# A small-tile pool moved to the bottom of SBUF, and ScalarE's work regrouped where two MLP phases meet

## The chip, the cores and the metric

The kernel runs on one core of a Trainium2 chip. The metric is the device time of one execution in microseconds (us). The engines are TensorE (PE; its weight loads, PEld, run beside the matmuls), VectorE (DVE), ScalarE (ACT), GpSimd (POOL) and SyncE (SP). On the last two mostly DMAs are issued; every engine works its own instructions off in order. On-chip memory (SBUF) has 128 partitions; an address below is a byte offset within a partition. Matmul results go to PSUM.

## The reference, cut to what matters

Two layers over 1024 tokens of width 1024, in float32. The change lies in the MLP of each layer; its pool edit moves operands of all matmuls.

```python
for i in range(DEPTH):                      # DEPTH = 2
    h = rms_norm(x, norm_mix_g[i])
    ...                                     # projections, convolution, retention
    x = x + mix                             # mix = [conv_out, ret_out] @ w_out[i]
    h = rms_norm(x, norm_ffn_g[i])
    x = x + jnp.square(jax.nn.relu(h @ w_ff1[i])) @ w_ff2[i]     # 1024 -> 4096 -> 1024
    h = rms_norm(x, norm_ple_g[i])
    x = x + jax.nn.sigmoid(h @ w_ple_gate[i]) * (p[i] @ w_ple_proj[i])
return rms_norm(x, final_norm_g)
```

## The kernel before

**Products.** Each float32 operand is split into a high part (rounded, made by ACT: `split`, L220) and a low part (the rest, made by DVE, L221), and a product is three matmuls (`mm3`, L252 to L254). A row of the profile such as `ps_mm<-h,s_hi` names the result, then the moving operand (512 columns that stream through the array), then the stationary one (128x128, loaded ahead).

**The MLP.** Both matrix products are done in 2x2 blocks by the seven-product (Strassen-Winograd) scheme. In the first phase `ff1_pair` makes a pair of hidden blocks at a time, p = 0 to 15: five products on sums of blocks of h and of the weights (two more were done early), then relu and square on ACT (L655, L656, the function `act`), then differences of the squared blocks on DVE, the *forms*, which go to DRAM by POOL (`store`, L658). The last pair, p = 15, belongs to a chunk that is done plainly later, and stores its squares only.

In the second phase `ff2_pairs` reads the forms back chunk by chunk (j = 0 to 6): `fetch` (L712, on POOL) brings the seven forms of a chunk into a ring of eleven tiles, and `ready` splits them on ACT and DVE. For each of four column groups g, `begin` does the first product into a PSUM tile p (`ps_ret`, two buffers), copies it to q on ACT (`copy(q, p)`, L744), and the other products go on from p, q and three further PSUM tiles e, y, r. The second product into p has to wait for that copy.

**The boundary.** While the last pair runs, `hook` already fetches chunk 0 and makes the first four of its forms ready. ACT therefore works on the last pair's squares, on chunk 0's splits, on the first weights of phase two and on the first `begin` in one queue.

**Who sets the order.** Instructions are written in the order of the code; a list scheduler then orders each engine's queue by priority. `issue_after(x)` adds the rule that the instructions of the block on x's engine stand behind x.

**Pools.** SBUF pools lie one above the other in the order in which they are opened: const, stage, w_hi, w_lo, h, tmp, small, and above these the pools of a stage, which are opened and closed (at, hx, s_hi, s_lo, ft; then form, acc; later pp, pr). small holds ten kinds of tiny tiles, three buffers each, padded to 32 bytes: 1,152 bytes, which is 4 x 256 + 128. In the built program stage begins at address 57,728 (225 x 256 + 128) and the pools of a stage at 153,088 (598 x 256). All tiles of stage, w_hi, w_lo, h and tmp are 2, 4 or 8 KB, so each of them begins 128 bytes past a multiple of 256; each tile of at, hx, s_hi, s_lo, ft, form, acc, pp and pr begins at a multiple of 256.

Of the kernel before, what the change touches and what calls it, by code (L numbers as in the profile page):

```python
# [43 lines left out]
PAIRS = D // (2 * P)  # L44
# [8 lines left out]
T_OUT, T_FF1, T_FF2, T_GATE, T_PROJ = 24, 32, 64, 96, 104  # L53
# [19 lines left out]
class _Trunk:  # L73
    def __init__(self, ctx, tc, x, xT, pT, pos, wts, vecs, convw, tabs, outT):
        self.tc, self.nc = tc, tc.nc
        self.x_tok, self.xT, self.pT, self.pos, self.wts = x, xT, pT, pos, wts
        self.vecs, self.convw, self.tabs, self.outT = vecs, convw, tabs, outT
        pool = lambda name, bufs, **kw: ctx.enter_context(tc.tile_pool(name=name, bufs=bufs, **kw))
        psum = bass.MemoryType.PSUM
        self.const = pool("const", 1)  # L80
        self.pools = {
            "stage": pool("stage", 2),
            "w_hi": pool("w_hi", 2),
            "w_lo": pool("w_lo", 2),
            "h": pool("h", 8),
            "tmp": pool("tmp", 2),
            "small": pool("small", 3),
            "ps_mm": pool("ps_mm", 5, space=psum),
            "ps_ret": pool("ps_ret", 2, space=psum),
            "ps_aux": pool("ps_aux", 1, space=psum),  # L90
        }

        self.small([P, 1], "pad")
        self.right = ctx.enter_context(ExitStack())
        self.norm_pools()
        self.dram = pool("dram", 1, space=bass.MemoryType.DRAM)
        self.low = {}
# [551 lines left out]
    def ff1_pair(self, L, p, xf, ws, e, early, forms, hook):  # L649
        nc, copy, add, sub = self.nc, self.nc.scalar.copy, self.nc.vector.tensor_add, self.nc.vector.tensor_sub  # L650
        t1, t2, t3, t4, q22 = xf
        w, sa, sb = ws

        def act(r, ps):
            nc.scalar.activation(r, ps, AF.Relu)  # L655
            nc.scalar.activation(r, r, AF.Square)  # L656

        store = lambda f, n, t: nc.gpsimd.dma_start(out=forms[p // 2][:, f:f + n, p % 2, :], in_=t)  # L658
        more = p + 1 < NPAIR
        b = self.tile("ps_mm")  # L660
        copy(b, e[0])  # L661
        self.product(b, sa, 0, t2, False, part=True)
        c = self.tile("ps_mm")
        copy(c, b)
        hook(p, 0)
        ps = self.tile("ps_ret")
        self.product(ps, sa, HT, t1, True)
        es = self.tile("tmp")
        copy(es, ps)
        hook(p, 1)  # L670
        if more:
            nxt = self.ff1_weights(L, p + 1)
            next(nxt)
            ne = self.early_load(p + 1, early)
        self.product(b, sb, 0, t3, False, part=True)
        qs = self.ft()
        q21, q22o = qs[:, 0, :], qs[:, 1, :]
        add(q22o, b, es)
        act(q22o, q22o)
        hook(p, 2)  # L680
        self.product(c, sb, HT, q22, False, part=True)
        q12 = es
        add(q12, c, es)
        act(q12, q12)
        hook(p, 3)
        if more:
            ws = next(nxt)
        self.product(b, w, HT, t4, False, part=True)
        act(q21, b)
        store(0, 2, qs)  # L690
        if p // 2 < WIDE:
            ta, tb = self.ft(), self.ft()
            sub(ta[:, 0, :], q12, e[1])
            sub(tb[:, 1, :], q22o, q12)
            sub(ta[:, 1, :], q22o, ta[:, 0, :])
            store(2, 2, ta)
            sub(tb[:, 0, :], q21, ta[:, 1, :])
            store(4, 2, tb)
        else:
            store(2, 1, q12)  # L700
        hook(p, 4)
        return (ws, ne) if more else None

    def slot(self):
        q = self.ring[self.turn % len(self.ring)]
# [24 lines left out]
            self.split(s, sh, sl)  # L730
        return (hi, lo), (sh, sl)

    def ff2_pairs(self, L, sources):
        nc, add, copy = self.nc, self.nc.vector.tensor_add, self.nc.scalar.copy
        acc_e, acc_h = (self.pools["acc"].tile([P, PAIRS, HT], F32, name="acc") for _ in range(2))
        self.acc = acc_e, acc_h

        def begin(j, g, ws):
            e = self.tile("ps_mm")
            if j:  # L740
                copy(e, acc_e[:, g, :])
            p, q = self.tile("ps_ret"), self.tile("ps_mm")
            self.product(p, ws[0], 2 * P, forms[0], True, part=True)
            copy(q, p)  # L744
            return e, p, q, ws[0], ws[1]

        weights = self.pair_weights(L, T_FF2)
        forms = self.coming
        now = begin(0, 0, weights)
        for j in range(WIDE):  # L750
            plain = j + 1 == WIDE
            for g in range(PAIRS):
                e, p, q, w, s = now
                q11, t1, t2, q21, t4, t3, q22 = forms
                end = g + 1 == PAIRS
                x11, x12 = self.x[2 * g]
                x21 = self.x[2 * g + 1][0]
                y = self.tile("ps_mm")
                copy(y, x21)
                self.product(e, s, 0, t1, j == 0, part=j > 0)  # L760
                copy(acc_e[:, g, :], e)
                if g == 0:
                    self.ready(*((4, 5, 6) if j == 0 else (6,)))
                    self.coming = []
                    self.fetch(sources[j + 1][:4])
                if end and not plain:
                    self.fetch(sources[j + 1][5:6])
                self.product(p, s, 2 * P, t2, False, part=True)
                r = self.tile("ps_mm")
                copy(r, p)  # L770
                if end and not plain:
                    self.fetch(sources[j + 1][6:7])
                self.product(q, w, 4 * P, q21, False, part=True)
                add(x11, x11, q)
                if 0 < g < 3:
                    self.ready(2 * g - 2)
                self.product(y, w, 6 * P, t4, False, part=True)
                copy(x21, y)
                if 0 < g < 3:
                    self.ready(2 * g - 1)  # L780
                if end and not plain:
                    self.ready(4)
                self.product(p, s, 4 * P, t3, False, part=True)
                if j:
                    add(acc_h[:, g, :], acc_h[:, g, :], p)
                else:
                    copy(acc_h[:, g, :], p)
                if end:
                    forms = self.coming
                if not (end and plain):  # L790
                    ng = (g + 1) % PAIRS
                    now = begin(j + end, ng, self.pair_weights(L, T_FF2 + PAIRS * (j + end) + ng))
                if g == 2 and not plain:
                    self.fetch(sources[j + 1][4:5])
                self.product(r, s, 6 * P, q22, False, part=True)
                add(x12, x12, r)
                if end and not plain:
                    self.ready(5)
        return self.coming
# [65 lines left out]
    def run(self):  # L865
# [8 lines left out]
        for L in range(DEPTH):  # L874
# [12 lines left out]
            with self.stage_pools(gen=16, conv_acc=4, ret=4, ctmp=3, rtmp=2, u=3):  # L887
# [15 lines left out]
                q = self.proj_qk(L, 0, hs, T_Q)  # L903
# [13 lines left out]
                q = self.proj_qk(L, 1, hs, T_Q)  # L917
# [11 lines left out]
            sources = []  # L929
            for j in range(NFB):  # L930
                q11 = early[j][:, :, 1, :]
                q21, q22s, t1s, t2s, t4s, t3s = (forms[j][:, f] for f in range(6))
                sources.append([q11, t1s, t2s, q21, t4s, t3s, q22s] if j < WIDE else [q11, q21, t1s, q22s])

            def hook(p, at):
                if p + 1 == NPAIR:
                    if at == 0:
                        self.fetch(sources[0][0:2])
                    elif at == 1:
                        self.fetch(sources[0][2:4])  # L940
                    elif at == 2:
                        self.fetch(sources[0][4:5])
                        self.ready(0)
                    elif at == 3:
                        self.fetch(sources[0][5:7])
                        self.ready(1)
                    else:
                        self.ready(2, 3)

            self.right_pools(ntmp=4, rstd=2)  # L950
            with self.stage_pools(at=2, hx=2, s_hi=2, s_lo=2):
                with self.stage_pools(ft=7):
# [24 lines left out]
                    now = ws, e  # L977
# [3 lines left out]
                        now = self.ff1_pair(L, p, (t1, t2, t3, t4, q22), *now, early, forms, hook)  # L981
                with self.stage_pools(form=1, acc=2):
                    self.ring[8] = self.pools["form"].tile([P, 4, HT], F32R, name="form")
                    f = self.ff2_pairs(L, sources)
                    self.norm_pools()
                    self.merge_pairs(0)
                    self.ff2(L, NFB - 1, 0, f[:2])
                    self.merge_pairs(1)
                    h3A = self.norm(0, v0 + V_PLE, SLACK)
                    self.ff2(L, NFB - 1, 1, f[2:])  # L990
# [94 lines left out]
```

## Time and profile before

| | before |
|---|---|
| median of three runs | 2378.33 us (2377.74 to 2378.80) |
| the profiled execution: its time / its span | 2378.69 us / 2376.7 us |
| PE busy | 2314.1 us, 97% of the span |
| DVE / ACT / POOL busy | 78% / 53% / 10% |
| mean granted TensorE clock | 0.994 of full speed |
| last pair of layer 0 ends, phase two begins | at about 748 us of the span |
| the same in layer 1 | at about 1919 us |

Time outside the span is 2.0 us. A busy PE is not a PE at its peak: a matmul's duration in a row (0.39 us) overlaps the next one's, so the pace is read from the distance of starts. A row of the timeline is: start, duration, engine, line, operation, `out<-in`, shapes, count, and in brackets the idle time of the engine just before and what ended it.

### The profile page before, as it was taken

The numbers are of one execution on the slowest core, as the hardware profiler recorded it, in microseconds if no ns is written. First come the engines' busy times: TensorE is split into PE (matmuls) and PEld (weight loads), VectorE is DVE, ScalarE is ACT, GpSimd is POOL, SyncE is SP. The second block draws the span as 40 slices with busy tenths as digits, with TensorE's granted clock in tenths as the row PEclk, the third lists the DMA queues.
The fourth block names the chain that finished last, engine by engine and source line by source line (L and its number), as shares of the span: only waits on it lengthen the run. The fifth ranks groups of instructions, "written<-read, shape, count | busy, mean of one in ns | idle before, by whom it ended". The sixth has DMA issues, their size and how long they took to land.

```text
span 2376.7 us, 29537 instructions
## 1 busy us (share of the span) xinstructions
PE 2314.1 (97%) x10548; PEld 1886.0 (79%) x10548; DVE 1857.8 (78%) x3262; ACT 1267.6 (53%) x2090; POOL 231.9 (10%) x364
## 2 busy tenths in 40 slices
PE   8999999999999999999999999999999999999998
PEld 7887887778887878788888888777788877777887
DVE  8999997376666677878999889845766667777788
ACT  5335237365556676736542352464655567676454
POOL 1000011001221101000000100100022111010000
PEclk9999999999999999999999999999999999999999
DMA  7644544666666444422265454555566654343324
GB/s 271 194 160 150 172 149 163 227 199 204 219 233 239 141 151 138 155 72 88 89 195 180 149 171 156 175 196 187 191 218 233 237 194 164 126 162 120 89 80 151
DMA packets 119171, 403.29 MB, mean 170 GB/s; under 512 B 13216, under 2 KB 21408, under 8 KB 119024
## 3 DMA queue, kind: packets, MB, share of 16 engines
q1 hardware_dynamic: 64032, 220.75, 30.5%
q0 software_dynamic: 43472, 157.59, 18.6%
q10 hardware_dynamic: 11520, 23.07, 2.6%
q8 instruction: 82, 1.34, 0.2%
q14 instruction: 65, 0.53, 0.1%
HBM read 295.46 MB, written 105.91 MB: 169 GB/s over the span
## 4 chain that ended last, share of the span: by engine, by line
PE 63%; issue 20%; DVE 8%; DMA 3%; POOL 3%; ACT 3%; POOLq 0%; DVEq 0%; ACTq 0%
PE ps_mm L252 19%; PE ps_mm L253 19%; PE ps_mm L254 19%; DVE conv_acc L411 2%; PE ps_ret L252 2%; PE ps_ret L254 2%; PE ps_ret L253 2%; POOL h L712 1%; DMA stage<-in_wts_dram 1%; DVE w_lo L221 1%; DVE h L221 1%; POOL gn_rs L546 1%; DMA w_lo<-low 1%; DMA h<-forms 1%; DVE ntmp L277 0%
## 5 line engine op out<-in xcount | busy, mean ns | idle before, releaser
L252 PE MATMUL ps_mm<-h,w_hi 128*128 128x512 f32 (+1 forms) x1584 | 615.2, 388 | 8.6 <-ACT w_hi L241 4.2
L254 PE MATMUL ps_mm<-h,w_lo 128*128 128x512 f32 (+1 forms) x1584 | 611.5, 386 | 2.9 <-DMA w_lo<-low 2.7
L253 PE MATMUL ps_mm<-h,w_hi 128*128 128x512 f32 (+1 forms) x1584 | 613.0, 387 | 0.0
L220 ACT CAST w_hi<-stage 128x1024 fp32r<-128x1024 f32 (+2 forms) x240 | 226.6, 944 | 300.1 <-PE ps_mm L253 169.7
L252 PEld LDWEIGHTS ps_mm<-h,w_hi 128*128 128x128 f32 x1584 | 299.2, 189 | 69.3 <-ACT w_hi L241 6.1
L254 PEld LDWEIGHTS ps_mm<-h,w_lo 128*128 128x128 f32 x1584 | 299.3, 189 | 62.8 <-DMA w_lo<-low 3.5
L253 PEld LDWEIGHTS ps_mm<-h,w_hi 128*128 128x128 f32 x1584 | 299.6, 189 | 56.1
L411 DVE SCALAR_TENSOR_TENSOR conv_acc<-u,cw,conv_acc 128x512 f32<-128x512 f32 x480 | 334.6, 746 | 0.9
L221 DVE TENSOR_TENSOR w_lo<-stage,w_hi 128x1024 fp32r<-128x1024 f32 (+2 forms) x240 | 261.1, 1088 | 51.0 <-ACT w_hi L220 50.3
L252 PE MATMUL ps_mm<-h,s_hi 128*128 128x512 f32 x400 | 158.9, 397 | 4.5 <-ACT ps_mm L661 4.5
L253 PE MATMUL ps_mm<-h,s_hi 128*128 128x512 f32 x400 | 158.5, 396 | 0.0
L254 PE MATMUL ps_mm<-h,s_lo 128*128 128x512 f32 x400 | 158.0, 395 | 0.0
L252 PE MATMUL ps_mm<-w_hi,h 128*128 128x512 f32 x384 | 150.6, 392 | 0.0
L253 PE MATMUL ps_mm<-w_lo,h 128*128 128x512 f32 x384 | 150.3, 391 | 0.0
L254 PE MATMUL ps_mm<-w_hi,h 128*128 128x512 f32 x384 | 150.2, 391 | 0.0
L241 ACT CAST w_hi<-stage 128x1024 fp32r<-128x1024 f32 x64 | 67.5, 1054 | 154.4 <-PE ps_mm L253 80.7
L270 ACT ACTIVATE ntmp<-x 128x256 f32<-128x256 f32 x208 | 81.1, 413 | 84.7 <-DVE ntmp L277 32.2
L252 PE MATMUL ps_ret<-h,s_hi 128*128 128x512 f32 x272 | 110.0, 405 | 16.5 <-ACT ps_mm L744 14.4
L221 DVE TENSOR_TENSOR s_lo<-ft,s_hi 128x1024 fp32r<-128x1024 f32 x64 | 78.4, 1225 | 52.7 <-ACT s_hi L220 52.7
L221 DVE TENSOR_TENSOR h<-h 128x1024 fp32r<-128x1024 f32 x76 | 92.6, 1222 | 30.8 <-ACT h L220 30.4
L254 PE MATMUL ps_ret<-h,s_lo 128*128 128x512 f32 x272 | 108.4, 398 | 0.0
L253 PE MATMUL ps_ret<-h,s_hi 128*128 128x512 f32 x272 | 108.0, 397 | 0.0
(267 smaller groups left out, 4310.1 us busy)
## 6 DMA issues: line engine op xcount, KB each, us to landing
stage<-in_wts_dram SPq DMA_DIRECT2D x336, 512.0 KB, 4.2
forms<-ft POOLq DMA_DIRECT2D x88, 512.0 KB, 6.2
low<-w_lo POOLq DMA_DIRECT2D x64, 512.0 KB, 5.2
w_lo<-low SPq DMA_DIRECT2D x64, 512.0 KB, 3.3
h<-forms POOLq DMA_DIRECT2D x62, 512.0 KB, 6.0
early<-at ACTq DMA_DIRECT2D x32, 512.0 KB, 4.4
at<-early POOLq DMA_DIRECT2D x30, 512.0 KB, 4.2
hx<-forms POOLq DMA_DIRECT2D x18, 512.0 KB, 5.7
```

The lines of the kernel that those rows point to most:

```text
L220: self.nc.scalar.copy(hi, src)
L221: self.nc.vector.tensor_sub(lo, src, hi.bitcast(F32))
L241: self.nc.scalar.copy(hi, st)
L252: mm(ps, lhsT=wh, rhs=xh, start=start, stop=False)
L253: mm(ps, lhsT=wh, rhs=xl, start=False, stop=False)
L254: mm(ps, lhsT=wl, rhs=xh, start=False, stop=stop)
L270: square = lambda k, out: nc.scalar.activation(out, self.x[k][h][:, cs], AF.Square)
L411: nc.vector.scalar_tensor_tensor(acc, u[:, j:j + HT], w(j), acc, ALU.mult, ALU.add)
L546: nc.gpsimd.tensor_tensor(rs, rs, self.npow[:, 0:HEADS], ALU.pow)
L712: self.nc.gpsimd.dma_start(out=f[1].bitcast(F32), in_=src)
```

## The change

1. The pool small is opened before stage instead of behind tmp. In the built program stage then begins at 58,880 (230 x 256), h at 83,456 (326 x 256); the pools of a stage stay at 153,088. Nothing else moves.
2. In the last pair, the square of q12, the relu and square of q21 and both their stores are taken out of `ff1_pair` and returned as a function `rest`. The other square, q22o, is stored alone at once (so two stores become three), and q21's square goes to a tile of the pool tmp instead of ft.
3. `ff2_pairs` calls `rest` behind its first `begin`, under `issue_after` the copy L744 (L758 in the change). Chunk 0's late forms, `ready(4, 5, 6)`, get the same rule.

```diff
         self.pools = {
+            "small": pool("small", 3),
             "stage": pool("stage", 2),
             "w_hi": pool("w_hi", 2),
             "w_lo": pool("w_lo", 2),
             "h": pool("h", 8),
             "tmp": pool("tmp", 2),
-            "small": pool("small", 3),
             "ps_mm": pool("ps_mm", 5, space=psum),
...
         q12 = es
         add(q12, c, es)
-        act(q12, q12)
+        if more:
+            act(q12, q12)
         hook(p, 3)
         if more:
             ws = next(nxt)
         self.product(b, w, HT, t4, False, part=True)
+        if not more:
+            store(1, 1, q22o)
+            hook(p, 4)
+
+            def rest():
+                act(q12, q12)
+                store(2, 1, q12)
+                q21 = self.tile("tmp")
+                act(q21, b)
+                store(0, 1, q21)
+
+            return rest
         act(q21, b)
         store(0, 2, qs)
...
-            copy(q, p)
-            return e, p, q, ws[0], ws[1]
+            copied = copy(q, p)
+            return copied, (e, p, q, ws[0], ws[1])
 
         weights = self.pair_weights(L, T_FF2)
         forms = self.coming
-        now = begin(0, 0, weights)
+        first, now = begin(0, 0, weights)
+        with self.tc.issue_after(first.ins):
+            rest()
...
                 if g == 0:
-                    self.ready(*((4, 5, 6) if j == 0 else (6,)))
+                    with self.tc.issue_after(first.ins):
+                        self.ready(*((4, 5, 6) if j == 0 else (6,)))
```

**ACT at the boundary of layer 0, before.** From the split of the third form of chunk 0 (t2s) on; L655 and L656 on tmp and ft are relu and square of q12 and q21, L744 is the first `copy(q, p)`, L759 the copy of y:

```order
L220 CAST h<-h 128x1024
L220 CAST s_hi<-at 128x1024
L655 ACTIVATE tmp<-tmp 128x512
L220 CAST h<-h 128x1024
L656 ACTIVATE tmp<-tmp 128x512
L655 ACTIVATE ft<-ps_mm 128x512
L220 CAST hx<-hx 128x1024
L656 ACTIVATE ft<-ft 128x512
L744 COPY ps_mm<-ps_ret 128x512
L759 COPY ps_mm<-x_97 128x512
L220 CAST h<-h 128x1024 x2
L220 CAST w_hi<-stage 128x768
```

**The same place after the change** (its lines are numbered 1 to 16 higher; L758 is the first `copy(q, p)`, L656 and L657 relu and square, L775 the copy of y, L777 that of acc, L787 that of r):

```order
L221 CAST h<-h 128x1024
L221 CAST s_hi<-at 128x1024
L221 CAST h<-h 128x1024
L221 CAST w_hi<-stage 128x768
L758 COPY ps_mm<-ps_ret 128x512
L656 ACTIVATE tmp<-tmp 128x512
L656 ACTIVATE tmp<-ps_mm 128x512
L657 ACTIVATE tmp<-tmp 128x512 x2
L775 COPY ps_mm<-x_97 128x512
L221 CAST hx<-hx 128x1024
L221 CAST h<-h 128x1024
L777 COPY acc<-ps_mm 128x512
```

Between the cast of `s_hi<-at` and the copy stood six instructions, and now two stand there: the split of the fourth form (`h<-h`) and the cast of group 1's weights (`w_hi<-stage`), which stood further down.

**PE at the same place, before.** The end of the first `begin`'s product (into `ps_ret`), the product into e (`ps_mm<-h,s_hi`, six matmuls), and the first matmul of the second product into p:

```order
L253 MATMUL ps_ret<-h,w_hi 128x512
L254 MATMUL ps_ret<-h,w_lo 128x512
L252 MATMUL ps_mm<-h,s_hi 128x512
L253 MATMUL ps_mm<-h,s_hi 128x512
L254 MATMUL ps_mm<-h,s_lo 128x512
L252 MATMUL ps_mm<-h,s_hi 128x512
L253 MATMUL ps_mm<-h,s_hi 128x512
L254 MATMUL ps_mm<-h,s_lo 128x512
L252 MATMUL ps_ret<-h,s_hi 128x512
```

**PE after the change**, from the same matmul on, with the tiles' numbers (`ps_ret_6543` is p of group 0, `ps_ret_6623` p of group 1, `w_hi_6616` the weights of group 1):

```order
L254 MATMUL ps_ret_6543<-h_3567,w_hi_6536 128x512
L255 MATMUL ps_ret_6543<-h_3567,w_lo_6537 128x512
L253 MATMUL ps_ret_6623<-h_3567,w_hi_6616 128x512
L254 MATMUL ps_ret_6623<-h_3567,w_hi_6616 128x512
L253 MATMUL ps_ret_6543<-h_3609,s_hi_6529 128x512
L254 MATMUL ps_ret_6543<-h_3609,s_hi_6529 128x512
L255 MATMUL ps_ret_6543<-h_3609,s_lo_6530 128x512
```

The scheduler has moved the product into e eleven matmuls down, and two matmuls of group 1's `begin` stand in its place. In layer 1 all queues change in the same way.

**POOL after the change**, from the last fetches of chunk 0 on (before, the two stores from tmp and ft, L658, stood between the fetch of `hx<-early_1` and both fetches `h<-forms_1`):

```order
L726 DMA h<-forms_0_3749 128x1024 x2
L659 DMA forms_7_3756<-ft 128x512
L726 DMA hx<-early_1_3742 128x2x512
L726 DMA h<-forms_1_3750 128x1024
L659 DMA forms_7_3756<-tmp 128x512 x2
L726 DMA form<-forms_1_3750 128x1024
```

The store of q22o went ahead of two fetches of chunk 1, and the other two stores behind them. On SP one weight load moves ahead of the two loads of per-layer inputs (L824) there.

## Rows read from the trace of the kernel before

**Rows 1.** The page: its first line, and the busy time of each engine (share of the span, instructions).

```profile
span 2376.7 us, 29537 instructions
PE 2314.1 (97%) x10548; PEld 1886.0 (79%) x10548; DVE 1857.8 (78%) x3262; ACT 1267.6 (53%) x2090; POOL 231.9 (10%) x364
```

**Rows 2.** Who PE waited for over the whole span: us in total, times, longest.

```profile
PE ps_ret L252 <- ACT ps_mm L744: 16.9, 12, 4.8
```

**Rows 3.** Timeline of PE at the boundary of layer 0.

```profile
748.71 0.40 PE L254 MATMUL ps_ret<-h,w_lo 128*128 128x512 f32 x1
...
750.33 0.40 PE L254 MATMUL ps_mm<-h,s_lo 128*128 128x512 f32 x1
755.53 0.80 PE L252 MATMUL ps_ret<-h,s_hi 128*128 128x512 f32 x1 [4.80 <-ACT ps_mm L744]
...
761.21 0.39 PE L253 MATMUL ps_mm<-hx,w_hi 128*128 128x512 f32 x1
```

**Rows 4.** The same at the boundary of layer 1.

```profile
1920.87 0.40 PE L254 MATMUL ps_mm<-h,s_lo 128*128 128x512 f32 x1
1925.96 0.79 PE L252 MATMUL ps_ret<-h,s_hi 128*128 128x512 f32 x1 [4.69 <-ACT ps_mm L744]
...
1932.03 0.39 PE L254 MATMUL ps_mm<-hx,w_lo 128*128 128x512 f32 x1
```

**Rows 5.** Timeline of ACT at the boundary of layer 0, from the relu of q12 to the copy that PE waits for, and the cast of group 1's weights.

```profile
750.96 0.62 ACT L655 ACTIVATE tmp<-tmp 128x512 f32<-128x512 f32 x1
751.49 1.03 ACT L220 CAST h<-h 128x1024 fp32r<-128x1024 f32 x1
752.43 0.63 ACT L656 ACTIVATE tmp<-tmp 128x512 f32<-128x512 f32 x1
752.96 0.57 ACT L655 ACTIVATE ft<-ps_mm 128x512 f32<-128x512 f32 x1
753.43 1.03 ACT L220 CAST hx<-hx 128x1024 fp32r<-128x1024 f32 x1
754.37 0.63 ACT L656 ACTIVATE ft<-ft 128x512 f32<-128x512 f32 x1
754.90 0.58 ACT L744 COPY ps_mm<-ps_ret 128x512 f32<-128x512 f32 x1
...
757.82 0.83 ACT L220 CAST w_hi<-stage 128x768 fp32r<-128x768 f32 x1
758.56 0.57 ACT L770 COPY ps_mm<-ps_ret 128x512 f32<-128x512 f32 x1
...
760.89 0.59 ACT L761 COPY acc<-ps_mm 128x512 f32<-128x512 f32 x1 [1.75 <-issue]
```

**Rows 6.** The same two instructions on ACT in layer 1: the relu of q12 and the copy.

```profile
1921.39 0.62 ACT L655 ACTIVATE tmp<-tmp 128x512 f32<-128x512 f32 x1
...
1925.34 0.58 ACT L744 COPY ps_mm<-ps_ret 128x512 f32<-128x512 f32 x1
```

[...]

```profile
[...]
[...]
[...]
```

**Rows 8.** Two shorter stalls of PE at the start of `ff1_pair` in each layer, and windows of the granted clock there.

```profile
525.41 0.63 PE L252 MATMUL ps_mm<-h,s_hi 128*128 128x512 f32 x1 [2.11 <-ACT ps_mm L661]
...
529.16 0.39 PE L252 MATMUL ps_mm<-h,s_hi 128*128 128x512 f32 x1
...
1697.59 0.50 PE L252 MATMUL ps_mm<-h,s_hi 128*128 128x512 f32 x1 [2.39 <-ACT ps_mm L661]
...
525.50:526.00 0.50, 0.50 (x2) 0.40 (x3) 0.50 (x1) 0.48 (x1) 0.00 (x0) 0.63 0.76 311
1694.00:1699.00 5.00, 2.61 (x12) 1.82 (x11) 5.00 (x8) 3.18 (x6) 0.55 (x1) 1.00 0.56 193
```

**Rows 9.** Timeline of PE in one pair of phase one of layer 0: the first matmul of five unbroken runs of one kind (12, then 24, 12 and 12 matmuls lie between these rows).

```profile
606.02 0.40 PE L252 MATMUL ps_mm<-h,w_hi 128*128 128x512 f32 x1
...
608.79 0.40 PE L252 MATMUL ps_mm<-h,s_hi 128*128 128x512 f32 x1
...
614.37 0.39 PE L252 MATMUL ps_mm<-hx,s_hi 128*128 128x512 f32 x1
...
617.11 0.40 PE L252 MATMUL ps_mm<-h,s_hi 128*128 128x512 f32 x1
...
619.90 0.40 PE L252 MATMUL ps_mm<-h,w_hi 128*128 128x512 f32 x1
```

**Rows 10.** Timeline of PE in the gated-input stage of layer 0: first and last matmul of two unbroken runs (90 matmuls `ps_mm<-pp`, then 141 matmuls `ps_mm<-h`).

```profile
1078.89 0.40 PE L254 MATMUL ps_mm<-pp,w_lo 128*128 128x512 f32 x1
...
1099.57 0.39 PE L254 MATMUL ps_mm<-pp,w_lo 128*128 128x512 f32 x1
...
1117.00 0.39 PE L252 MATMUL ps_mm<-h,w_hi 128*128 128x512 f32 x1
...
1148.73 0.39 PE L254 MATMUL ps_mm<-h,w_lo 128*128 128x512 f32 x1
```

**Rows 11.** Timeline of POOL at the boundary of layer 0: the store of q21 and q22o.

```profile
755.29 0.72 POOL L658 DMA_DIRECT2D forms<-ft  x1 [1.37 <-ACT ft L656]
```

More of the change, by code (lines that the diff above doesn't have):

```diff
@@ L701, in ff1_pair @@
         hook(p, 4)
-        return (ws, ne) if more else None
+        return ws, ne
     def slot(self):
@@ L731, in pair_weights, with ff2_pairs @@
         return (hi, lo), (sh, sl)
-    def ff2_pairs(self, L, sources):
+    def ff2_pairs(self, L, sources, rest):
         nc, add, copy = self.nc, self.nc.vector.tensor_add, self.nc.scalar.copy
@@ L791, in ff2_pairs @@
                     ng = (g + 1) % PAIRS
-                    now = begin(j + end, ng, self.pair_weights(L, T_FF2 + PAIRS * (j + end) + ng))
+                    _, now = begin(j + end, ng, self.pair_weights(L, T_FF2 + PAIRS * (j + end) + ng))
                 if g == 2 and not plain:
@@ L983, in run @@
                     self.ring[8] = self.pools["form"].tile([P, 4, HT], F32R, name="form")
-                    f = self.ff2_pairs(L, sources)
+                    f = self.ff2_pairs(L, sources, now)
                     self.norm_pools()
```

## The prediction

> **What bounds the kernel now.** The page first: PE is busy for 2314.1 of 2376.7 us, DVE for 1857.8 and ACT for 1267.6 [rows 1]. PE is the bound nearly everywhere, and an edit can save time in two ways only: a shorter idle stretch of PE, or matmuls that follow each other faster. So I read two kinds of view. The list of waits says where PE stands still for ACT: the copy L744 held it for 16.9 us in 12 places, the longest 4.8 us [rows 2]. The timeline of PE puts two of them at the boundaries, 4.80 and 4.69 us [rows 3, 4], which leaves 16.9 − 4.80 − 4.69 = 7.4 us for the ten others, at the later chunks' starts. For the second way I read distances of starts in unbroken runs of one kind of matmul [rows 9, 10]; the edit of the pools changes nothing else on PE than addresses.
>
> **The change, part by part.**
>
> *1. The pool.* It removes no instruction and adds none; the stage pools stay where they are and stage, w_hi, w_lo, h and tmp move up by 1,152 bytes. Before, a tile of h or w begins 128 bytes past a multiple of 256 and a tile of hx, form, pp, s_hi or s_lo at one, so a matmul whose moving and stationary tiles come from the two groups is *mixed*. Counted in the built program, 2,544 of the 9,312 matmuls with 512 columns are mixed: `h,s` 2,016, `hx,w` 240, `pp,w` 192, `form,w` 96. After it none is.
>
> Do mixed ones run slower? In one pair of phase one, `h,w` takes (608.79 − 606.02)/12 = 0.2308 us from start to start, `h,s` (614.37 − 608.79)/24 = 0.2325, `hx,s` (617.11 − 614.37)/12 = 0.2283, and `h,s` again (619.90 − 617.11)/12 = 0.2325 [rows 9]. The mixed kind is the slowest both times, with the same three lines in the same rhythm. In the gated-input stage, `pp,w`, mixed, takes (1099.57 − 1078.89)/89 = 0.2324 and `h,w`, not mixed, (1148.73 − 1117.00)/140 = 0.2266 [rows 10]. So the mixed pitch is 0.2324 to 0.2325 everywhere, and the other 0.2266 to 0.2308. The price of being mixed is 1.7 ns against `h,w` and 4.2 against `hx,s` in phase one, 5.8 in the gated-input stage. I take the mean, 3.9 ns: 2,544 × 0.0039 = 9.9 us. The bounds are 2,544 × 0.0017 = 4.3 and 2,544 × 0.0058 = 14.8, and zero if the cause is something else (first rival).
>
> [...]
>
> *2. The boundary.* Before it, ACT works from 750.96 through six instructions (relu of q12, a split of h, square, relu of q21, the split of hx, square), and the copy L744 starts at 754.90 [rows 5]; PE's second product into p waits until 755.53 [rows 3]. After it, between the same point and the copy stand the split of h and the cast w_hi. The split takes 751.49 to 752.43 until the next starts, 0.94 us, and the cast 0.83 us (0.74 to the next start) [rows 5]. So the split runs from 750.96, the cast from 751.90 to 752.73, and the copy from 752.64 to 753.22, 754.90 − 752.64 = 2.26 us earlier.
>
> PE's order is different as well. The product into e, six matmuls from behind 748.71 to 750.33, which lies before the stall now, moves behind it: 6 × 0.2317 = 1.39 us of work no longer cover the wait (0.2317 us is the full-clock pitch at the boundary, in between those of rows 9). In its place stand two matmuls of group 1, which need the cast. PE thus goes on when the cast ends, at about 752.78 (0.05 us for the signal), with two matmuls, and the copy at 753.22 is then done almost as they are. The gain is 755.53 − 752.78 − 1.39 = 1.36 us. In layer 1 the same starting point is 1921.39 [rows 6]: 1921.39 + 0.94 + 0.83 + 0.05 = 1923.21, and 1925.96 − 1923.21 − 1.39 = 1.36. The stalls become less short than the 2.75 us by which they end earlier, since without e they begin earlier too: in layer 0 at 748.71 + 0.40 = 749.11, so 3.67 us; in layer 1, with the same 1.62 us less ahead, 1923.21 − (1921.27 − 1.62) = 3.56 (1921.27 is the end of the row at 1920.87).
>
> Then the clock. [...] What does a stall of 3.6 to 3.7 us cost? Two shorter ones bound it: after 2.11 us at 525.41 the clock was down (0.63), and 9 gaps took 3.75 instead of 2.09, a loss of 1.66; around the 2.39 us at 1697.59 the window has 1.00 and there was no loss [rows 8]. I take 1.66, since the new stall is nearer to the long ones than to the one without loss: gains of 1.01 and 1.17. Bounds: the loss stays as it is (nothing), or it is gone (5.50).
>
> Sum of the boundaries: 1.36 + 1.01 + 1.36 + 1.17 = 4.9 us; from 2.7 to 2.7 + 5.5 = 8.2.
>
> *3. What the faster pitch gives back.* The ten stalls at chunk starts end when ACT's copy is there, not when PE arrives. If the matmuls ahead of them, in phase two, are faster by 1.2 us in all, the stalls lengthen by it: I put 0.12 us on each of the ten, +1.2 us. Bounds: 0 (ACT is released by PE, so its copies come earlier too) and 3.9, at which phase two would return its whole share.
>
> *4. Costs put at nothing.* ACT's amount of work is unchanged: what stood before the copy stands behind it, while PE has the second product and e to do; in the old order ACT was ahead of PE from there on. The square of q21 goes to tmp instead of ft, same shape. POOL gets one store more per layer. Its stores waited, the first for 1.37 us until 755.29 [rows 11]; now q22o's goes out ahead of two fetches, and the other two behind them when ACT has made their squares. If that cover is gone, the fetches behind them come late; but these are chunk 1's, wanted only when chunk 0 is done. The copy into acc waited for 1.75 us at 760.89 on something that is no engine [rows 5], the store out of ft by the time; with that store issued earlier the wait should shrink, and PE doesn't depend on it. SP's loads of per-layer inputs wait for tiles of tmp, which two squares now hold longer; a weight load goes ahead of them, and the next weights are wanted later still.
>
> **Sum.** − 9.9 − 4.9 + 1.2 = − 13.6, from the profiled execution's own time, 2378.69: 2365.1. That execution lies 0.36 us above the median, so 2364.7 against the median; I say 2365.
>
> **The rivals.**
>
> *The pitch follows something else than the address.* Mixed operands also lie in different regions of SBUF, and `h,s` is work whose stationary tiles come from a sum made on DVE, other traffic than `h,w`. If kind and not place is the cause, 9.9 and 1.2 fall away: 2378.33 − 4.9 = 2373.5. [...] Against it: `hx,s` has the same kind of stationary tile and is the fastest in [rows 9].
>
> *The boundary gives nothing.* ACT has the same work, only later; the stall moves to the next copy from p or to the acc copy, or the e product behind it waits. Then − 9.9 + 1.2 = − 8.7, 2369.6. For it: ACT copies g = 1's p at 758.56 [rows 5], behind the moved instructions. Against it: ACT itself waits for 1.75 us at 760.89 [rows 5], which is slack for what is moved behind the copy.
>
> *Neither does anything*: about 2378.
>
> *Slower: aligned tiles are the slow case.* The slow pitch 0.2324 could belong to a conflict that all matmuls get once every tile starts at a multiple of 256, and `hx,s`, both low in that sense, be fast for another reason. Then the other 9,312 − 2,544 = 6,768 matmuls pay 0.0039 us each, + 26.4, and with the boundary's gain the time is 2378.33 + 26.4 − 4.9 = 2400. The mixed ones stay slow in it. It decides from the point where more than 4.9/0.0039 = 1,256 matmuls become slow. Against it: `hx,s`, at multiples of 256 on both sides today, has 0.2283 [rows 9].
>
> **How the numbers follow.** The forecast of both terms 0.58; pool without effect 0.22; boundary without effect 0.10; neither 0.06; slower 0.04. Within the forecast the bounds of the terms run from − 14.8 − 8.2 = − 23 to − 4.3 − 2.7 + 3.9 = − 3.1; both ends at once are unlikely, and I let it go from 2357 (the price at 5.8 ns with the boundary at 3 to 8) to 2372. The range 2357 to 2375 takes in the two cases with one half without effect and leaves out neither, slower, and the forecast's outermost ends, together under 2 in 10. A measurement of this kernel tells from no change about 0.2%, 4.8 us. Faster by more, under 2373.6: the forecast nearly whole, the case without the boundary, and half of the case without the pool: 0.56 + 0.10 + 0.12 = 0.78. Slower 0.05, the rival and a little of what nobody named. Same 0.17.
>
> **What the changed profile would show.** Pool: in phase one `h,s` runs from start to start in 0.228 to 0.231 us instead of 0.2325, and `pp,w` in 0.227 instead of 0.2324; if they keep 0.232, the first term falls. Boundary: PE's idle stretch is 3.5 to 3.7 us, ended by the cast w_hi or the copy L758, and starts about 1.4 us earlier; the copy starts at about 752.6 less what the pitch has brought by then. [...] Giving back: the waits for L758 at later chunk starts sum to 7.4 to 9 us. The prediction is wrong if the chunk starts lengthen by more, if the next wait for ACT behind the boundary takes up the 1.36 us, or if matmuls that were not mixed become slower.

## The result and the profile after

| | before | after |
|---|---|---|
| median of four runs | 2378.51 us (2377.74 to 2378.80) | 2360.57 us (2357.94 to 2365.54) |
| ratio of after to before | | 0.9928 (95% interval 0.9910 to 0.9945) |
| the profiled execution's span | 2376.7 us | 2356.2 us |

17.9 us faster by the medians, where 13.3 were forecast. The profiled execution is the fastest of the four. One of the five executions of e8 below took 5938 us and is left out of its figures.

The page of after, the rows that answer to [rows 1]:

```profile
span 2356.2 us, 29545 instructions
PE 2295.5 (97%) x10548; PEld 1883.6 (80%) x10548; DVE 1855.8 (79%) x3262; ACT 1265.9 (54%) x2090; POOL 232.5 (10%) x366
```

PE has the same 10,548 instructions and is busy for 18.6 us less (2314.1 to 2295.5). So most of the gain is not idle time that went, but matmuls that follow each other faster.

**The pitch** (the distance from the start of one matmul to the start of the next). The timeline of PE in the same pair of phase one as in [rows 9], in after:

```profile
605.10 0.39 PE L253 MATMUL ps_mm<-h,w_hi 128*128 128x512 f32 x1
...
607.82 0.39 PE L253 MATMUL ps_mm<-h,s_hi 128*128 128x512 f32 x1
...
613.26 0.39 PE L253 MATMUL ps_mm<-hx,s_hi 128*128 128x512 f32 x1
...
615.98 0.39 PE L253 MATMUL ps_mm<-h,s_hi 128*128 128x512 f32 x1
...
618.70 0.39 PE L253 MATMUL ps_mm<-h,w_hi 128*128 128x512 f32 x1
```

Every run of 12 takes 2.72 us, 0.2267 us from start to start: `h,s` (before 0.2325) below the forecast 0.228 to 0.231, but also `h,w` (0.2308) and `hx,s` (0.2283), which were not mixed. The pair of 60 matmuls takes 13.60 us instead of 619.90 − 606.02 = 13.88. In the gated-input stage `pp,w` comes to (1088.23 − 1067.36)/92 = 0.2268 from the fourth matmul of its run on, as forecast (0.227; before 0.2324 [rows 10]):

```profile
1067.36 0.39 PE L253 MATMUL ps_mm<-pp,w_hi 128*128 128x512 f32 x1
...
1088.23 0.39 PE L255 MATMUL ps_mm<-pp,w_lo 128*128 128x512 f32 x1
```

**The boundary.** PE at the boundary of layer 0, then of layer 1, in after (answering to [rows 3, 4]):

```profile
744.98 0.39 PE L255 MATMUL ps_ret<-h,w_lo 128*128 128x512 f32 x1
748.77 0.67 PE L253 MATMUL ps_ret<-h,w_hi 128*128 128x512 f32 x1 [3.40 <-ACT w_hi L221]
...
752.22 0.45 PE L253 MATMUL ps_mm<-h,w_hi 128*128 128x512 f32 x1
...
1904.02 0.50 PE L254 MATMUL ps_ret<-h,w_hi 128*128 128x512 f32 x1 [0.76 <-DVE h L222]
...
1909.13 0.53 PE L253 MATMUL ps_ret<-h,w_hi 128*128 128x512 f32 x1 [3.67 <-ACT w_hi L221]
...
1912.88 0.40 PE L254 MATMUL ps_mm<-h,w_hi 128*128 128x512 f32 x1
```

The stalls are 3.40 and 3.67 us (forecast 3.67 and 3.56) and end with the cast w_hi, as forecast. In before the granted clock falls while PE stands still, to means of 0.82 and 0.60 in the half microseconds at 754.0 and 1925.0; it reads 0.50 from 756 to 760 and from 1926 to 1931, and in the half microsecond at 761.0 it is back to a mean of 0.85 (after the window its length, then PE, PEld, DVE, ACT and POOL busy; the number behind POOL's is the granted clock, 1.00 being full speed):

```profile
754.00:754.50 0.50, 0.00 (x0) 0.00 (x0) 0.47 (x3) 0.50 (x2) 0.00 (x0) 0.82 0.02 8
761.00:761.50 0.50, 0.50 (x4) 0.39 (x3) 0.44 (x1) 0.50 (x2) 0.17 (x1) 0.85 1.06 434
1925.00:1925.50 0.50, 0.00 (x0) 0.00 (x0) 0.50 (x2) 0.50 (x2) 0.00 (x0) 0.60 1.00 385
```

In after the granted clock behind the stalls is 0.52 in the mean from 748.77 to 752.22 (0.50 from 749 to 752) and 0.54 from 1909.13 to 1912.88 (0.50 from 1910 to 1912): 8 gaps take 752.22 − 748.77 = 3.45 us instead of 8 × 0.2267, a loss of 1.64, and 9 gaps take 3.75, a loss of 1.71 (1.66 was taken). In layer 1 another wait of 0.76 us, for a form of chunk 0, stands ahead of the stall, which before does not have.

ACT there (answering to [rows 5]): the copy has moved up to right behind the split and the cast.

```profile
746.94 1.04 ACT L221 CAST h<-h 128x1024 fp32r<-128x1024 f32 x1
747.89 0.83 ACT L221 CAST w_hi<-stage 128x768 fp32r<-128x768 f32 x1
748.62 0.57 ACT L758 COPY ps_mm<-ps_ret 128x512 f32<-128x512 f32 x1
```

From split to copy it is 748.62 − 746.94 = 1.68 us, by the forecast 0.94 + 0.74 = 1.68. The list of waits has the copy L758 now with 7.4 us in 9 places, where ten chunk starts had 7.4 before [rows 2]:

```profile
PE ps_ret L253 <- ACT ps_mm L758: 7.4, 9, 1.3
PE ps_ret L253 <- ACT w_hi L221: 7.1, 2, 3.7
```

### The profile page after: what moved, and what is told of

It reads as the page before. It is cut to its first block, busy times and chain, and to the rows that moved or that the text cites. A ratio compares the mean times of both kernels' runs of the same rounds, so it can differ in the third digit from the quotient of the medians.

```text
span 2356.2 us, 29545 instructions
## 1 busy us (share of the span) xinstructions
PE 2295.5 (97%) x10548; PEld 1883.6 (80%) x10548; DVE 1855.8 (79%) x3262; ACT 1265.9 (54%) x2090; POOL 232.5 (10%) x366
## 3 DMA queue, kind: packets, MB, share of 16 engines
q0 software_dynamic: 43504, 157.59, 18.6%
## 4 chain that ended last, share of the span: by engine, by line
PE 61%; issue 20%; DVE 8%; DMA 5%; ACT 3%; POOL 3%; POOLq 0%; SPq 0%; DVEq 0%; ACTq 0%
PE ps_mm L253 18%; PE ps_mm L255 18%; PE ps_mm L254 18%; DVE conv_acc L412 2%; PE ps_ret L253 1%; PE ps_ret L254 1%; PE ps_ret L255 1%; DMA stage<-in_wts_dram 1%; POOL h L726 1%; DVE w_lo L222 1%; DMA h<-forms 1%; POOL gn_rs L547 1%; DVE h L222 1%; DMA w_lo<-low 1%; DMA hx<-forms 1%
```

## The experiments

Two edits make four kernels: before, after, and each edit alone. Theory A says that the pitch follows the addresses of a matmul's two operands, by their remainders by 256; K, that it follows the kind of work; R, that the place of small or the distances between pools count, and not the remainder by 256.

**e1: the pool edit alone.** The kernel before with

```diff
         self.pools = {
+            "small": pool("small", 3),
             "stage": pool("stage", 2),
...
             "tmp": pool("tmp", 2),
-            "small": pool("small", 3),
```

> The kernel before with the pool small opened first, and nothing else. If the pitch of the matmuls follows the addresses (theory A), nearly all of the gain that is not the boundary's is here: about 17.9 - 4.9 = 13 us less than before, 2365.5 us, with 0.2267 us from start to start in the runs ps_mm<-h,s_hi of phase one. If the kind of work sets the pitch (theory K), no change (2378.5 us, 0.2325 us).

Measured: 0.9934 (0.9922 to 0.9946) of before, 15.7 us less on the scale of 2378.5 (12.8 to 18.6). K falls.

**e2: the boundary alone.** The change with small left behind tmp.

> The change without its pool edit: small stays behind tmp, only the boundary's order is new. By the prediction's second term 4.9 us less than before, 2373.6 us, with h,s at 0.2325 us as before; 2378.5 if the stall only moves on; 2366 or less if the boundary and not the pool was the main part of the gain.

Measured: 0.9979 (0.9970 to 0.9989), 5.0 us less (2.6 to 7.1).

**e3: the kernel before, shifted by 128 bytes.** Small stays behind tmp.

```diff
+        self.const_up = pool("const_up", 1)
...
-        self.npow = const.tile([P, 8], F32, name="npow")
+        self.npow = self.const_up.tile([P, 8], F32, name="npow")
```

and the same for halfpi, posi and posf; const_up is opened behind tmp.

> The kernel before, small still behind tmp, but four constants of 32 bytes each move from below stage to above tmp: stage, w_hi, w_lo, h and tmp move down by 128 bytes instead of up by 1,152, and nothing becomes mixed any more. Theory A: as the pool edit alone, about 2365.5 us and h,s at 0.2267 us. If it is the place of small that counts, or its distance from the stage's pools (theory R), or the kind of work (K): 2378.5 us and 0.2325 us.

Measured: 0.9933 (0.9920 to 0.9945), the same as e1, with another distance, another place of small, and stage at 57,600 = 225 x 256.

**e4: the changed kernel, shifted back by 128 bytes** with the same edit.

> The changed kernel, small at the bottom, with the same four constants moved from below stage to above tmp: stage to tmp begin 128 bytes past a multiple of 256 again, so the matmuls mixed before are mixed again. Theory A: only the boundary's gain is left, 2378.5 - 4.9 = 2373.6 us, h,s at 0.2325 us. Theory R: as the changed kernel, 2360.6 us, h,s at 0.2267 us.

Measured: 0.9978 (0.9968 to 0.9989), the same as e2. R falls in both directions: what is left in common is the remainder. The windows of phase one of layer 0, in which PE has no idle time, count the matmuls for e1 and e3, then for e4 and e2 (after the window its length, PE busy and in brackets its instructions, then PEld, DVE, ACT, POOL):

```profile
540.00:740.00 200.00, 200.00 (x884) 165.59 (x883) 135.94 (x195) 114.45 (x174) 41.48 (x62) 1.00 0.68 229
```

```profile
540.00:740.00 200.00, 200.00 (x883) 165.40 (x882) 135.16 (x193) 113.58 (x173) 41.51 (x62) 1.00 0.68 230
```

```profile
540.00:740.00 200.00, 200.00 (x866) 162.54 (x865) 134.04 (x191) 113.33 (x173) 39.91 (x59) 1.00 0.66 221
```

```profile
540.00:740.00 200.00, 200.00 (x866) 162.54 (x865) 134.72 (x192) 113.73 (x173) 39.26 (x58) 1.00 0.66 220
```

884 or 883 matmuls where nothing is mixed, 866 where `h,s` is, at a granted clock of 1.00 in all four: 2% of the phase, and it isn't the clock.

**e5: TensorE alone.** run(m, s, n) issues n matmuls one behind the other, with four blocks of the moving tile m and eight of the stationary tile s in turn.

```diff
+        run(mv0, st[0], 96)
+        for d in range(0, 257, 32):
+            run(mv0, st[d], 96)
+        run(mv128, st[0], 96)
+        run(mv128, st[128], 96)
+        run(mv128, st[64], 96)
...
```

> The reference's work is left out: TensorE alone runs 512-column float32 matmuls in unbroken runs of 96, the moving tile mv_0 at a multiple of 256, the stationary tile st_d d bytes past one (d = 0, 32, ..., 224, 256), then mv_128 with st_0, st_128 and st_64, then runs of 12 that alternate: mv_0 with st_128 and mv_0 with st_0, and mv_128 with st_0 and mv_0 with st_0. No other engine works meanwhile. Theory A (the addresses of the two operands alone): 0.2267 us from start to start for d = 0, for d = 256 and for mv_128 with st_128, 0.2325 for d = 128 and for mv_128 with st_0; where the other d lie is open. If the difference needs other engines' accesses to SBUF (theory C), all runs have one pitch. Alternating runs: 0.2267 and 0.2325 in turn if each matmul pays for itself; above 0.2267 in the aligned ones if a mixed run slows its neighbours, as the runs h,w (0.2308) and hx,s (0.2283) of before would have it.

The trace's names leave numbers out, so the runs are told by their order. Each row below is one stretch inside one run: its start, the time from the first start to the last end, and the count; the pitch is (time − 0.39)/(count − 1). In order st_0, 32, 64, 96, 128, 160, 192, 224, 256 with mv_0, then mv_128 with st_0, st_128, st_64:

```profile
32.73 19.66 PE L904 MATMUL ps_mm<-mv,st 128*128 128x512 f32 x86
54.75 19.53 PE L904 MATMUL ps_mm<-mv,st 128*128 128x512 f32 x83
76.69 20.70 PE L904 MATMUL ps_mm<-mv,st 128*128 128x512 f32 x88
99.78 19.61 PE L904 MATMUL ps_mm<-mv,st 128*128 128x512 f32 x83
121.78 20.39 PE L904 MATMUL ps_mm<-mv,st 128*128 128x512 f32 x87
143.64 20.69 PE L904 MATMUL ps_mm<-mv,st 128*128 128x512 f32 x88
166.73 19.61 PE L904 MATMUL ps_mm<-mv,st 128*128 128x512 f32 x85
188.73 19.53 PE L904 MATMUL ps_mm<-mv,st 128*128 128x512 f32 x83
210.63 19.66 PE L904 MATMUL ps_mm<-mv,st 128*128 128x512 f32 x86
232.64 20.69 PE L904 MATMUL ps_mm<-mv,st 128*128 128x512 f32 x88
255.72 19.66 PE L904 MATMUL ps_mm<-mv,st 128*128 128x512 f32 x86
276.82 19.39 PE L904 MATMUL ps_mm<-mv,st 128*128 128x512 f32 x84
```

0.2267 us where both operands have the same remainder by 256 (*aligned*: st_0, st_256, and mv_128 with st_128: 19.27/85), and 0.2326 to 0.2344 where they differ by 32, 64, 96, 128, 160 or 224; 0.2288 for st_192 and 0.2289 for mv_128 with st_64, which is the same difference. Nothing else worked meanwhile (from 33 to 52, 55 to 74 and 144 to 164 us DVE, ACT and POOL are busy for 0.00 us, the DMA share is 0.00 and the granted clock 1.00): theory C falls. No other difference is free, and 128 is one among several.

The alternating runs of 12: the starts of an aligned run, the mixed one behind it, the next aligned one and the next mixed one; first where the stationary tile changes, then (last three rows) where the moving one does.

```profile
300.43 0.40 PE L904 MATMUL ps_mm<-mv,st 128*128 128x512 f32 x1
303.20 0.40 PE L904 MATMUL ps_mm<-mv,st 128*128 128x512 f32 x1
305.99 0.40 PE L904 MATMUL ps_mm<-mv,st 128*128 128x512 f32 x1
308.75 0.40 PE L904 MATMUL ps_mm<-mv,st 128*128 128x512 f32 x1
...
333.75 0.39 PE L904 MATMUL ps_mm<-mv,st 128*128 128x512 f32 x1
336.49 0.40 PE L904 MATMUL ps_mm<-mv,st 128*128 128x512 f32 x1
339.28 0.39 PE L904 MATMUL ps_mm<-mv,st 128*128 128x512 f32 x1
```

The mixed runs take 2.79 us (0.2325). The aligned ones take 2.76 to 2.77 behind a mixed one with another stationary tile (0.230 to 0.231) and 2.74 behind one with another moving tile (0.2283), where 12 × 0.2267 would be 2.72. These are the figures of `h,w` (0.2308) and `hx,s` (0.2283) in [rows 9]: a mixed run also slows the matmuls behind it. In the trace the delay sits at the start of the aligned run. In the one at 305.99 the first seven distances take 1.62 us instead of 1.59 and the next four 0.91, which is undisturbed; in the one at 333.75 the first three take 0.70 instead of 0.68 and the other nine 2.04, undisturbed.

**e6 and e9: the product into e first again.** The changed kernel, with group 1's weights put behind the copy and PE's order mended (self.last is the last matmul that was written, here the last one into e, then into p):

```diff
-                self.product(p, s, 2 * P, t2, False, part=True)
+                order = lambda: self.tc.issue_after(self.last.ins) if j == g == 0 else nullcontext()
+                with order():
+                    self.product(p, s, 2 * P, t2, False, part=True)
...
-                self.product(q, w, 4 * P, q21, False, part=True)
+                with order():
+                    self.product(q, w, 4 * P, q21, False, part=True)
...
-                    _, now = begin(j + end, ng, self.pair_weights(L, T_FF2 + PAIRS * (j + end) + ng))
+                    with self.tc.issue_after(first.ins) if j == g == 0 else nullcontext():
+                        ws = self.pair_weights(L, T_FF2 + PAIRS * (j + end) + ng)
+                    _, now = begin(j + end, ng, ws)
```

> The changed kernel with two more edits at the boundary: the cast of group 1's weights is put behind the copy L758 on ACT, and on PE the product into e is put back ahead of the second product into p. By the changed kernel's rows the copy then starts at the end of the split of h, 747.89, ends at 748.46, and PE has done 1.39 us of e in the idle time: 748.77 - 748.50 + 1.39 = 1.66 us a layer earlier, an idle stretch of 1.75 instead of 3.40 us, and no lowered clock behind it, another 1.6: 3.2 a layer, 6.4 us less than the changed kernel in all, about 2354 against 2378.5 of before. If the stall moves to the next wait for ACT instead, 0 to 3 us less.

Measured: 0.9902 (0.9890 to 0.9915), 6.2 us less than the changed kernel's 0.9928 (6.4 expected), and rows of PE's stalls at layer 0's boundary in e6:

```profile
747.39 0.50 PE L253 MATMUL ps_ret<-h,s_hi 128*128 128x512 f32 x1 [0.76 <-ACT ps_mm L758]
...
750.93 0.50 PE L253 MATMUL ps_mm<-hx,w_hi 128*128 128x512 f32 x1 [0.53 <-ACT hx L221]
...
752.20 0.50 PE L254 MATMUL ps_mm<-hx,w_hi 128*128 128x512 f32 x1 [0.76 <-DVE hx L222]
```

The long stall is down to 0.76 us, the granted clock from 747 to 748 reads 1.00, and new, short waits stand behind it. To compare with the changed kernel on one chip:

> The changed kernel once more, beside the next two on one chip. 0.9928 of before; if the boundary's new order adds to the pool's gain as e1 and e2 have it (0.9934 and 0.9979), 0.9913.

> e6 once more, beside the changed kernel. By the traces 2 x (3.40 - 0.76 + 1.6) us, less the waits for the form hx that it has and the changed kernel has not (0.53 + 0.76 a layer): 5.9 us, 0.25%, less than the changed kernel. If the difference between e6 and the changed kernel was one of chips, both have the same ratio.

Measured: the changed kernel 0.9918 (0.9903 to 0.9932), 2360.42 us, nearer to the sum 0.9913 than to 0.9928, with both in its interval; e9 0.9902 (0.9886 to 0.9917), 2356.86 us. Medians 3.6 us apart (5.9 expected), all runs of e9 (up to 2357.70) below all of the changed kernel's (from 2358.97); the intervals of the ratios overlap, so the gain over the changed kernel is likely and its size open.

**e7: the fourth form behind the copy too.**

```diff
-                        self.ready(2, 3)
+                        self.ready(2)
...
         with self.tc.issue_after(first.ins):
+            self.ready(3)
             rest()
```

> As the run before, and the split of chunk 0's fourth form (q21) also goes behind the copy L758. The copy starts at the end of the cast s_hi, 746.94, ends at 747.51: another 0.95 us a layer earlier. But the third product, into q, needs that split's result and DVE's low part behind it, at about 749.5, and PE reaches it at 748.9: it gives 0.4 to 0.6 back. So 7 to 8 us less than the changed kernel, about 2353; if the wait for the fourth form costs more than 0.95, it is slower than the run before.

Measured: 0.9928 (0.9915 to 0.9941), slower than e6 and no faster than the changed kernel, where 7 to 8 us less were expected. The wait for the fourth form is short, but a later one, for the copy of r, became 1.85 us long:

```profile
748.74 0.50 PE L254 MATMUL ps_mm<-h,w_hi 128*128 128x512 f32 x1 [0.27 <-DVE h L222]
...
755.06 0.50 PE L253 MATMUL ps_ret<-h,s_hi 128*128 128x512 f32 x1 [1.85 <-ACT ps_mm L790]
```

ACT had the same work ahead of that copy as in e6, so what PE won at the first wait it lost at this one; whether that is all of the difference isn't shown. In layer 1 the granted clock also fell behind this wait, to 0.65 in the mean of 1920 to 1924 (last section).

**e10: the form hx earlier.** As e6, with rest() and the late forms in another order:

```diff
-                        self.ready(*((4, 5, 6) if j == 0 else (6,)))
+                        if j == 0:
+                            self.ready(4)
+                            rest()
+                        self.ready(*((5, 6) if j == 0 else (6,)))
```

> As e6, and chunk 0's fifth form (hx) is split right behind the copy of y, ahead of the last pair's relus and squares. The two waits for hx of e6, 0.53 and 0.76 us in layer 0, go: 2.6 us less than e6 in both layers. If the copy of r (L789), for which PE waited 0.70 us in e6, comes later by what PE comes earlier, nothing.

Measured: 0.9929 (0.9916 to 0.9941), 2363.93 us, 7 us slower than e9 beside it, where 2.6 us less or nothing was expected. The waits for hx are gone, and the time stands in one piece before group 1's weights, which ACT casts where it did:

```profile
752.91 0.50 PE L253 MATMUL ps_ret<-h,w_hi 128*128 128x512 f32 x1 [2.66 <-ACT w_hi L221]
...
754.31 0.79 PE L255 MATMUL ps_ret<-h,w_lo 128*128 128x512 f32 x1 [0.66 <-DVE w_lo L222]
```

Windows of the granted clock (the number behind POOL's) in e10, then in e6:

```profile
754.00:756.00 2.00, 1.69 (x4) 1.40 (x5) 1.82 (x3) 2.00 (x4) 0.00 (x0) 0.50 0.82 284
756.00:758.00 2.00, 2.00 (x6) 1.52 (x6) 1.74 (x2) 0.78 (x2) 0.00 (x0) 0.50 0.85 270
```

```profile
754.00:756.00 2.00, 1.26 (x4) 0.78 (x5) 2.00 (x3) 2.00 (x4) 0.00 (x0) 1.00 0.92 363
```

e10 falls to 0.50 behind its stall, where from 755.33 to 759.17 nine gaps take 0.427 us each; e6, whose idle time there is cut into pieces of 0.4 to 0.8 us, stays at 1.00.

## Why the prediction was right

The direction, the cause of the pool's gain, the shorter stalls and the time within its range were right; the likeliest time, 2365, was 4 us too high, since the pool's term was too small. The clock's part of the boundary came out in the changed profile by luck. Point by point:

- **Pool.** Right in its cause: e1 and e3 (0.9934 and 0.9933) against e2 and e4 (0.9979 and 0.9978), and e5, show that the addresses of moving and stationary tile decide. In e5, with no other engine at work, the pitch still depends on how the two operands' addresses lie to each other: 0.2267 us aligned, 0.2326 and 0.2333 where they differ by 128. The term was mis-sized: 9.9 us was forecast, 15.7 measured (e1). The step that failed is the price of 3.9 ns, a mean over three comparisons of which two were made with `h,w` and `hx,s` of phase one as if these ran undisturbed. They were slowed by their mixed neighbours (e5), so the price came out too small, and their own loss was not counted at all. With the undisturbed 5.8 ns of [rows 10] the mixed ones give 2,544 × 0.0058 = 14.8; the neighbours add, in phase one, 13.88 − 13.60 − 36 × 0.0058 = 0.07 us a pair, 2.2 us in 32 pairs. The sum of 17.0, an estimate, lies within e1's interval (12.8 to 18.6), and so it does less the 2 us or so that chunk starts give back (below).
- **Boundary.** Right in the copy's place on ACT, the wait that takes its place (the cast w_hi) and the length of the stalls: 2.96 to 3.73 us, 3.41 in the mean, in the four profiles of the new order (after, e8, e2, e4), 4.62 to 4.80 in the three of the old one (before, e1, e3). The sum fits too: 4.9 us forecast, 5.0 measured in e2 and 5.2 in e4 (0.9978). But no run shows its clock part, 1.01 + 1.17 us. These are the losses at the boundaries of before (13 gaps in 5.68 us instead of 3.01, a loss of 2.67, and 14 in 6.07 instead of 3.24, a loss of 2.83, by 0.2317 us a gap; together the 5.50 of the bounds) less the 1.66 taken for a shorter stall; what the runs show behind the shorter stall are losses of 1.64 and 1.71 (after) and 2.68 (e8, layer 1). Windows of 12 us around the boundary of layer 0 in after and of layer 1 in e8 and e1 (the granted clock is the number behind POOL's; with the 0.50 that e10's windows read behind its stall, an estimate from the mean gives 12 × 0.28/0.50 = 6.7 us at the lowered clock for 0.72, and 3.4 us for 0.86):

```profile
745.00:757.00 12.00, 8.60 (x31) 6.64 (x30) 9.87 (x12) 10.72 (x16) 3.95 (x7) 0.86 0.98 343
1908.00:1920.00 12.00, 8.65 (x26) 6.57 (x26) 9.12 (x10) 10.13 (x16) 3.96 (x7) 0.72 0.95 345
1908.00:1920.00 12.00, 7.34 (x26) 6.01 (x27) 9.91 (x12) 10.97 (x17) 2.92 (x5) 0.86 0.78 281
```

  Here e8 is the changed kernel again, and in layer 1 it loses 2.68 us behind its stall of 3.35 (13 gaps take 5.63). e1 has the old order, and in layer 1 it loses 1.47 behind 4.75 (7 gaps take 3.06). Such windows read 0.72 at both boundaries of before, 0.86 at both of e1 and one of each in e3; with the new order 0.86 at both of after, 0.72 at both of e4 and one of each in e2 and e8. So the smaller loss does not go with the shorter stall, and the 1.64 and 1.71 of after, against 2.67 and 2.83 before, were luck. What the profiles show is the stalls' part: 4.73 − 3.41 = 1.3 us a layer, 2.6 in all, where the forecast took 2.7. Whether the clock adds to it over many executions stays open: the intervals of e2 (2.6 to 7.1) and e4 (2.6 to 7.6) hold 2.7 as well as 4.9, and with nothing mixed the new order adds 1.4 us (after against e1) to 3.8 (e8 against e1).
- **Giving back.** 1.2 us was forecast. Without the two boundary stalls the waits for this copy sum to 7.4 us in before, 6.8 in e2 and 5.9 in e4, where `h,s` is mixed, and to 11.5 in e1, 8.0 in e3, 7.4 in after and 9.0 in e8, where nothing is. That is 2.3 us more in the mean, but after and e8, the same kernel, already differ by 1.6, so the term stays open between 0 and 4.
- **Costs at nothing.** From 748.77 to 755.93 and from 1909.13 to 1918 PE in after has no further idle time, so nothing that was moved behind the copy came late there. The 0.76 us at 1904.02 stands ahead of the stall; e4 has two such waits in layer 1, and e8, before, e1 and e3 have none. Whether the change brings them isn't shown.
- **The rivals.** The pool without effect falls with e1 and e3, the boundary without effect with e2 and e4; that aligned tiles are the slow case falls with the first row of e5: 0.2267 us is the fastest pitch in it.

## What to carry to other kernels

Look at the remainder by 256 of the addresses of both operands of a matmul: where pools of odd size (padding, tiny tiles) lie between them, a stretch of 128 bytes was worth 0.7% of this kernel (e1 0.9934, e3 0.9933), and moving four constants did as much as moving the pool. Read a pitch from long unbroken runs of one kind, since here runs of 12 carried their neighbours' delay (0.2283 to 0.2308 us instead of 0.2267). When a stall can't be removed, cut it into pieces with work that is ready: at this boundary all waits from 2.66 us (e10) to 4.80 us (before) in one piece went with a lowered clock (0.72 or 0.86 in the mean of the 12 us around, 0.50 behind the stall in e10), pieces of 0.4 to 0.9 us did not (the granted clock is 1.00 from 747 to 756 in e6, and in e9 it is 1.00 from 747 to 748 and the pitch behind the pieces 0.23 us), and making the one piece shorter, 3.4 us instead of 4.7, did not do away with it.

## What the runs showed of the hardware that was not expected

- The pitch of 512-column float32 matmuls depends on the operands' relative address, with PE alone at work: 0.2267 us for a difference of 0 by 256, 0.2288 for 192, 0.2326 to 0.2344 for 32, 64, 96, 128, 160 and 224 (e5).
- The delay reaches past the mixed run: a run of 12 aligned ones behind it takes 20 to 50 ns too long (e5).
- Short stalls don't lower the clock alike: in e7 PE waits for the copy of r for 1.85 us in both layers, at 755.06 and at 1920.08. Behind the first the granted clock stayed at 1.00, behind the second it fell:

```profile
1920.08 0.49 PE L253 MATMUL ps_ret<-h,s_hi 128*128 128x512 f32 x1 [1.85 <-ACT ps_mm L790]
755.00:759.00 4.00, 3.94 (x17) 3.25 (x18) 3.20 (x4) 2.54 (x5) 0.00 (x0) 1.00 0.73 231
1920.00:1924.00 4.00, 3.92 (x11) 3.11 (x12) 4.00 (x5) 4.00 (x7) 0.00 (x0) 0.65 0.87 301
```

What decides it the runs don't show.
